# A two-layer trunk on one core: order of vector work at the start of each FFN, two sums of weights formed by an adding DMA, and one negative mean less per norm

## The chip, the cores and the metric

One core of a Trainium2 chip runs the whole program in one launch. The metric is the device time in microseconds (us). Three runs of the kernel before gave 2072.91, 2076.62 and 2079.84 us; the median is 2076.62.

## The reference, cut to what matters

Batch 1, 512 tokens, width 1024, float32, two layers. Each layer is a half-step SwiGLU FFN, a token mixer (layer 0: native sparse attention, NSA; layer 1: the gated linear recurrence HGRN2), and a second half-step FFN. A post-norm follows each of the six blocks:

```
for i in range(2):
    x = layer_norm(alpha*x + 0.5*swiglu(x, w_gate1, w_up1, w_down1))
    x = layer_norm(alpha*x + mixer_i(x))
    x = layer_norm(alpha*x + 0.5*swiglu(x, w_gate2, w_up2, w_down2))
swiglu(x, g, u, d) = (silu(x @ g) * (x @ u)) @ d        # 1024 -> 2816 -> 1024
```

## The kernel before, in words

Tokens lie in four chunks of 128 (c = 0 to 3); the model width in eight slices of 128 (k). Matmuls run in the fp32r format, and to keep float32 accuracy each operand is split into a high part (a rounded copy, made by ScalarE, line 123) and a low part (the difference, made by VectorE, line 124). A product of two split operands is three matmuls (`mm3`, lines 140 to 142). x stands transposed in SBUF as `xh` and `xl`.

The order of TensorE's instructions is the order of the code. The order on VectorE, ScalarE, GpSimd and in the DMA queues is made by a planner that lists the instructions by their place in the code and by when it thinks that they can start. The helper `after(ins)` tells the planner that what is traced inside it comes behind `ins` on the engine of each of `ins`.

**A norm** (`ln_tok`, lines 216 to 243) takes chunk c: two adds to x with bn_stats (lines 223, 224), bn_aggr (225), the negative mean `nm`, named lm, on GpSimd (227), 1/sqrt(var) by two GpSimd instructions (212, 213), and then the two half rows. The second half of chunks 0 to 2 goes through ScalarE (which takes `nm` as its bias) and GpSimd; everything else is two VectorE instructions per half (238, 239). In chunk 3 nothing reads `nm`. `finish` (245) runs the last matmuls of a block chunk by chunk with the norms behind them, and transposes chunks 0 and 1 for the next block meanwhile; chunks 2 and 3 stay in `pending` and are flushed by the next block.

**An FFN** (`ffn_body`, line 273) has 11 pairs of 128-column blocks of gate and up weights. Pair 0 is done plainly (`plain_pair`): first all products with tokens of chunks 0 and 1, in four parts, with the flush (transpose on TensorE, high part on ScalarE, low part on VectorE: `to_xt`) of chunk 2 ahead of the third part and of chunk 3 ahead of the fourth; then all products with chunks 2 and 3. Pairs 1 to 10 are done by `seven`: a Strassen-like scheme with 7 instead of 8 block products. It needs sums of blocks of x (`token_forms`, lines 189 to 200: four VectorE instructions of 128x512 for each of chunks 2 and 3, traced right behind the low part in `to_xt`, then split into t0, t1, t2) and sums of weight blocks. For pair g the gate and up weights come by four DMAs of 512 KB into two `fr` tiles (three buffers), called r0 and r1 here; a00, a10 are the column halves of r0 and a01, a11 those of r1. VectorE makes three sums into `raw` tiles (three buffers, shared with all weights that are loaded raw) and one in place, all at line 387:

```
s3 = a00 - a10;  s1 = a10 + a11;  s2 = a11 - s3 (into a10);  t = a01 - s2
w1 = parts(a00), w7 = parts(s3), w6 = parts(s2), w2 = parts(a01)
w5 = parts(s1),  w4 = parts(a11), w3 = parts(t)
```

`parts` is the split into high and low part. TensorE then takes products 1, 7, 6, 2, 5, 4, 3. Product 3 adds into bank e, which `c = e + p1` on VectorE (line 442) must have read first. The next pair's r1 needs an `fr` buffer of this pair; the last reader of both is the sum t. In the first FFN alone, pair 1's vector and scalar instructions already stand behind the flush of chunk 3.

Of the kernel before, what the change touches and what calls it, by code (L numbers as in the profile page):

```python
# [10 lines left out]
F32 = mybir.dt.float32  # L11
# [4 lines left out]
ALU = mybir.AluOpType  # L16

P = 128
# [3 lines left out]
NT = T // P  # L22
# [23 lines left out]

NSTD = 1

PLACE = 64

PSC = 4
# [10 lines left out]
class Trunk:  # L62
    def __init__(self, ctx, tc, a):
        self.tc, self.nc, self.a = tc, tc.nc, a
        nc = self.nc
        self.cst = ctx.enter_context(tc.tile_pool(name="cst", bufs=1))
        self.act = ctx.enter_context(tc.tile_pool(name="act", bufs=1))
        self.ident = self.cst.tile([P, P], F32, name="ident")
        make_identity(nc, self.ident)

        self.gap(self.cst, 128)
        self.mhalf = self.cst.tile([P, NT], F32, name="mhalf")
        nc.vector.memset(self.mhalf, -0.5)
        self.x = [self.act.tile([P, D], F32, name=f"x{c}") for c in range(NT)]

        self.raw = ctx.enter_context(tc.tile_pool(name="raw", bufs=3, reuse_waits="tile"))
        self.wr = ctx.enter_context(tc.tile_pool(name="wr", bufs=5, reuse_waits="tile"))
        self.xt = None
        self.pending = {}
        self.nxt, self.early, self.forms = None, [], None  # L80

    def gap(self, pool, n):
        pool.tile([P, n // 4], F32, name="gap")
# [93 lines left out]
    def to_xt(self, c):  # L177
        for h in range(2):
            p = self.psum().rearrange("p (k t) -> p k t", k=4)
            for j in range(4):  # L180
                k = 4 * h + j
                self.nc.tensor.transpose(p[:, j, :], self.x[c][:, k * P : (k + 1) * P], self.ident)
            s, t = slice(4 * h, 4 * h + 4), slice(c % 2 * P, c % 2 * P + P)
            ins = self.split(self.xh[:, c // 2, s, t], self.xl[:, c // 2, s, t], p)
            if self.forms is not None and c >= 2:
                self.token_forms(h, t, p)
        return ins

    def token_forms(self, h, t, p):
# [26 lines left out]
    def ln_tok(self, c, banks, gb, eps, out=None, scale=1.0):  # L216
        nc = self.nc
        x = self.x[c]
        st = self.small.tile([P, 2, 6], F32, name="st", tag="st")
        mv = self.small.tile([P, 2], F32, name="mv", tag="mv")  # L220
        for h in range(2):
            s = slice(512 * h, 512 * h + 512)
            nc.vector.scalar_tensor_tensor(x[:, s], x[:, s], float(scale), banks[h], op0=ALU.mult, op1=ALU.add)  # L223
            nc.vector.bn_stats(st[:, h, :], x[:, s])  # L224
        nc.vector.bn_aggr(mv, st.rearrange("p a b -> p (a b)"))
        nm = self.small.tile([P, 1], F32, name="lm", tag="lm")
        nc.gpsimd.tensor_scalar(nm, mv[:, 0:1], -1.0, None, op0=ALU.mult)
        r = self.rsqrt(mv[:, 1:2], 1, eps)
        for h in range(2):
            s = slice(512 * h, 512 * h + 512)  # L230

            if h == 1 and c < NT - 1:
                nc.scalar.activation(x[:, s], x[:, s], AF.Identity, bias=nm)
                nc.scalar.activation(x[:, s], x[:, s], AF.Copy, scale=r)
                nc.gpsimd.tensor_tensor(x[:, s], x[:, s], gb[0][:, s], op=ALU.mult)
                nc.gpsimd.tensor_tensor(x[:, s], x[:, s], gb[1][:, s], op=ALU.add)
            else:
                nc.vector.scalar_tensor_tensor(x[:, s], x[:, s], mv[:, 0:1], gb[0][:, s], op0=ALU.subtract, op1=ALU.mult)
                nc.vector.scalar_tensor_tensor(x[:, s], x[:, s], r, gb[1][:, s], op0=ALU.mult, op1=ALU.add)
            if out is not None:  # L240
                nc.sync.dma_start(out[0, c * P : (c + 1) * P, s], x[:, s])
        if out is None:
            self.pending[c] = partial(self.to_xt, c)
# [29 lines left out]
    def ffn_body(self, pool, wg, wu, wd, gb_idx, out):  # L273
        nc = self.nc
        self.gap(pool, 128)
        h = pool.tile([P, 12, T], F32, name="h")

        self.wx = pool, 2
        w3 = [w.rearrange("(k p) f -> p k f", p=P) for w in (wg, wu)]
        LASTU = 4  # L280
        with ExitStack() as es:
            mid = es.enter_context(self.tc.tile_pool(name="mid", bufs=1, reuse_waits="tile"))
            self.gap(mid, 192)
            tf = [[mid.tile([P, 4, 256], F32R, name=f"t{n}{x}") for x in "hl"] for n in range(3)]

            hq = h.rearrange("p j t -> p (j t)")
            xb = hq[:, 2048:4096].rearrange("p (a k t) -> p a k t", a=2, k=4)
            f1, f2 = (hq[:, 1024 * n : 1024 * n + 1024].rearrange("p (k t) -> p k t", k=4) for n in (4, 5))
            for half, (f0, nf) in enumerate(((0, 12), (12, 10))):
                for pr in range(nf // 2):  # L290
                    g = f0 // 2 + pr
                    if g < NSTD:
                        if g == 0:
                            for k in range(2):
                                ks = slice(4 * k, 4 * k + 4)
                                nc.vector.tensor_tensor(xb[:, k], self.xh[:, 0, ks].bitcast(F32), self.xl[:, 0, ks].bitcast(F32), op=ALU.add)
                            self.forms = xb, f1, f2
                        self.plain_pair(mid, w3, g, h[:, 2 * pr : 2 * pr + 2, :])
                        if g == 0:
                            self.forms = None  # L300
                            for (hi, lo), src in zip(tf, (f1, f2, xb[:, 0])):
                                self.split(hi, lo, src)
                        if g == NSTD - 1:
                            self.split(self.xh[:, 1, 0:4], self.xl[:, 1, 0:4], xb[:, 1])
                    else:

                        with self.after(self.flushed if g == NSTD and gb_idx == (0, 0) else ()):
                            self.seven(mid, tf, w3, g, h[:, 2 * pr : 2 * pr + 2, :], 1 if g < NSTD + 2 else 2 if half == 1 and pr == 0 else 0)
                if half == 0:
                    banks = self.down(wd, h, f0, nf, nf, None)  # L310
                    for c in range(NT):
                        for x in range(2):
                            s = slice(512 * x, 512 * x + 512)
                            nc.vector.scalar_tensor_tensor(self.x[c][:, s], self.x[c][:, s], 2.0 * ALPHA, banks[c][x], op0=ALU.mult, op1=ALU.add)
        with ExitStack() as es:
            wl = es.enter_context(self.tc.tile_pool(name="wl", bufs=4, reuse_waits="tile"))
            gb = self.ln_params(*gb_idx, [wl.tile([P, D], F32, name=n, bufs=1) for n in ("lng", "lnb")])
            banks, last = self.down(wd, h, f0, nf, nf - LASTU, wl)
            self.finish(last, banks, gb, 4.0 * LN_EPS, out)
# [49 lines left out]
    def seven(self, pool, tf, w3, g, h, wide):  # L369
# [3 lines left out]
        nc = self.nc  # L373
# [3 lines left out]
        for kk in range(2):  # L377
            t = pool.tile([P, 2, 4, 256], F32, name="fr", tag="fr", bufs=3)
# [3 lines left out]
        a00, a10, a01, a11 = r[0][..., :P], r[0][..., P:], r[1][..., :P], r[1][..., P:]  # L382

        def form(x, y, op, out=None):
            if out is None:
                out = self.raw.tile([P, 2, 4, P], F32, name="raw", tag="raw")
            tt(out, x, y, op=op)  # L387
            return out
# [8 lines left out]

        w = {1: parts(a00)}
        s3 = form(a00, a10, ALU.subtract)
        s1 = form(a10, a11, ALU.add)  # L400
        s2 = form(a11, s3, ALU.subtract, a10)
        w[7] = parts(s3)
        w[6] = parts(s2)
# [16 lines left out]
        c = pool.tile([P, 2, 2, 256], F32, name="c")  # L420
# [841 lines left out]
def body(ctx, tc, a, out):  # L1262
# [14 lines left out]

    for r, t.nxt, t.place in zip(run, first[1:] + [None], (PLACE, 0, 0, PLACE, 0, 0)):
        r()
# [25 lines left out]
```

## Time and profile before

| what | us |
|---|---|
| runs, median of 3 (lowest, highest) | 2076.62 (2072.91, 2079.84) |
| the profiled execution, its own time | 2074.36 |
| its span from first to last instruction | 2072.6 |

The profiled execution lies 2.26 us under the median of the runs. In the span TensorE is shown busy for 99%, at full clock (mean granted 0.999). The four FFNs start at about 9, 703, 1046 and 1730 us.

How to read it: times in rows are us from the span's start. In a timeline a row is start, duration, engine, line, operation, out<-in, shapes, count, and in brackets the idle time before it with what ended it. Merged rows (x2) carry the start of the first. VectorE instructions overlap by some 0.08 us, so back-to-back ones start 0.60 us (128x512) or 1.14 us (128x1024) apart while the row says 0.68 or 1.22.

### The profile page before, as it was taken

Reading aid. Unit: us, or ns where it says so; the run is one execution under the profiler, and the core shown is the slowest. Engines: PE = TensorE matmul, PEld = TensorE weight load, DVE = VectorE, ACT = ScalarE, POOL = GpSimd, SP = SyncE. Lnnn points to the kernel's source line nnn. Section 1 sums busy time; section 2 is a strip of 40 time slices with the busy share of each in tenths; the row PEclk is TensorE's granted clock in tenths of the full one; section 3 lists DMA queues with packets and bytes.
Section 4 is the critical chain, followed back from the end, with each engine's and each line's share of the span. In section 5 each row is a group of like instructions: output and inputs, shape, how many; then the busy total and the mean of one; then the engine's idle time right before and its main releaser. Section 6 shows DMA issues by size and latency. Waiting matters only on the chain.

```text
span 2072.6 us, 34647 instructions
## 1 busy us (share of the span) xinstructions
PE 2045.6 (99%) x14329; PEld 1879.6 (91%) x14329; DVE 1402.1 (68%) x2108; ACT 988.2 (48%) x1594; POOL 197.1 (10%) x313
## 2 busy tenths in 40 slices
PE   9999999999999999999999999999999999999998
PEld 9998998889999899899899989988888989998996
DVE  8846865367776796486598468654647859855864
ACT  5543552355665355255345435524736735542551
POOL 0000002001112200000110000030421212000002
PEclk9999999999999999999999999999999999999999
DMA  5341342341101145133234413523230022442331
GB/s 183 123 149 56 103 144 74 89 111 34 40 32 52 62 123 163 41 103 106 97 102 131 145 51 102 163 63 96 88 119 31 2 72 76 130 162 61 103 123 41
DMA packets 138762, 194.00 MB, mean 94 GB/s; under 512 B 8571, under 2 KB 117435, under 8 KB 138604
## 3 DMA queue, kind: packets, MB, share of 16 engines
q1 hardware_dynamic: 138604, 191.79, 29.8%
q8 instruction: 112, 1.84, 0.4%
q14 instruction: 46, 0.38, 0.1%
HBM read 189.58 MB, written 2.19 MB: 93 GB/s over the span
## 4 chain that ended last, share of the span: by engine, by line
PE 84%; DVE 9%; ACT 3%; POOL 2%; issue 1%; DMA 1%; SPq 0%; POOLq 0%; DVEq 0%; ACTq 0%
PE ps L140 23%; PE ps L142 23%; PE ps L141 23%; PE po L851 3%; PE ps L835 2%; DVE wlo L124 1%; PE ps L1187 1%; PE ps L356 1%; DVE raw L387 1%; DMA fr<-in_ffn_w_up_dram 1%; DVE st L224 1%; PE sc L803 1%; PE sc L802 1%; DVE x L223 1%; PE ps L574 1%
## 5 line engine op out<-in xcount | busy, mean ns | idle before, releaser
L124 DVE TENSOR_TENSOR wlo<-raw,whi 128x1024 fp32r<-128x1024 f32 (+1 forms) x253 | 311.2, 1234 | 259.7 <-ACT whi L123 259.2
L123 ACT ACTIVATE whi<-raw 128x1024 fp32r<-128x1024 f32 (+1 forms) x253 | 265.9, 1056 | 335.7 <-PE ps L142 157.0
L141 PE MATMUL ps<-xl,whi 128*128 128x256 f32 (+1 forms) x992 | 293.6, 296 | 2.7 <-DVE xl L124 2.7
L140 PE MATMUL ps<-xh,whi 128*128 128x256 f32 (+1 forms) x992 | 294.5, 297 | 1.1 <-ACT xh L123 0.5
L142 PE MATMUL ps<-xh,wlo 128*128 128x256 f32 (+1 forms) x992 | 293.2, 296 | 0.0
L142 PE MATMUL ps<-whi,xlo 128*128 128x512 f32 x704 | 274.5, 390 | 1.5 <-DVE xlo L124 1.5
L140 PE MATMUL ps<-whi,xhi 128*128 128x512 f32 x704 | 274.5, 390 | 0.0
L141 PE MATMUL ps<-wlo,xhi 128*128 128x512 f32 x704 | 274.0, 389 | 0.0
L141 PEld LDWEIGHTS ps<-xl,whi 128*128 128x128 f32 x992 | 186.8, 188 | 9.9 <-DVE xl L124 3.5
L140 PEld LDWEIGHTS ps<-xh,whi 128*128 128x128 f32 x992 | 186.6, 188 | 8.7 <-ACT xh L123 1.0
L142 PEld LDWEIGHTS ps<-xh,wlo 128*128 128x128 f32 x992 | 186.3, 188 | 6.4
L123 ACT ACTIVATE whi<-fr 128x1024 fp32r<-128x1024 f32 x120 | 126.7, 1061 | 129.7 <-PE ps L141 80.4
L140 PE MATMUL ps<-xh,xhi 128*128 128x256 f32 x640 | 177.8, 278 | 3.1 <-DVE c L442 3.1
L124 DVE TENSOR_TENSOR wlo<-fr,whi 128x1024 fp32r<-128x1024 f32 x120 | 146.1, 1219 | 46.7 <-ACT whi L123 46.7
L141 PE MATMUL ps<-xl,xhi 128*128 128x256 f32 x640 | 177.5, 277 | 0.0
L142 PE MATMUL ps<-xh,xlo 128*128 128x256 f32 x640 | 177.4, 277 | 0.0
L387 DVE TENSOR_TENSOR raw<-fr 128x1024 f32<-128x1024 f32 x120 | 145.8, 1219 | 21.7 <-DMA fr<-in_ffn_w_up_dram 20.3
L142 PEld LDWEIGHTS ps<-whi,xlo 128*128 128x128 f32 x704 | 132.2, 188 | 30.6 <-DVE xlo L124 3.2
L141 PEld LDWEIGHTS ps<-wlo,xhi 128*128 128x128 f32 x704 | 132.2, 188 | 27.0
L140 PEld LDWEIGHTS ps<-whi,xhi 128*128 128x128 f32 x704 | 132.2, 188 | 26.8
L124 DVE TENSOR_TENSOR xlo<-h,xhi 128x1024 fp32r<-128x1024 f32 x44 | 53.9, 1226 | 112.8 <-ACT xhi L123 112.8
L140 PEld LDWEIGHTS ps<-xh,xhi 128*128 128x128 f32 x640 | 120.4, 188 | 3.7 <-DVE c L442 3.7
(270 smaller groups left out, 4865.5 us busy)
## 6 DMA issues: line engine op xcount, KB each, us to landing
raw<-in_ffn_w_down_dram SPq DMA_DIRECT2D x88, 512.0 KB, 3.5
fr<-in_ffn_w_gate_dram SPq DMA_DIRECT2D x80, 512.0 KB, 4.0
fr<-in_ffn_w_up_dram SPq DMA_DIRECT2D x80, 512.0 KB, 5.1
raw<-in_hgrn_w_in_dram SPq DMA_DIRECT2D x32, 512.0 KB, 4.1
raw<-in_nsa_w_in_dram SPq DMA_DIRECT2D x18, 512.0 KB, 4.0
raw<-in_ffn_w_gate_dram SPq DMA_DIRECT2D x8, 512.0 KB, 5.3
raw<-in_ffn_w_up_dram SPq DMA_DIRECT2D x8, 512.0 KB, 4.7
raw<-in_nsa_w_out_dram SPq DMA_DIRECT2D x8, 512.0 KB, 3.5
```

The costliest lines, as they stand in the source:

```text
L123: a = self.nc.scalar.activation(hi, src, AF.Copy)
L124: b = self.nc.vector.tensor_tensor(lo, src, hi.bitcast(F32), op=ALU.subtract)
L140: mm(out, l[0], r[0], start=start, stop=False)
L141: mm(out, l[0], r[1], start=False, stop=False)
L142: mm(out, l[1], r[0], start=False, stop=stop)
L223: nc.vector.scalar_tensor_tensor(x[:, s], x[:, s], float(scale), banks[h], op0=ALU.mult, op1=ALU.add)
L224: nc.vector.bn_stats(st[:, h, :], x[:, s])
L356: nc.tensor.matmul(out, l, xx, start=k == low == 0 and xx is x[0], stop=k == 7 and low == 1)
L387: tt(out, x, y, op=op)
L574: nc.tensor.matmul(ph, w1[:, j, :], self.ap(z[:, 0:1], 2 * j, [[16, 129]]), start=j == 0, stop=j == 15)
L835: nc.tensor.transpose(p[:, j * P : j * P + P], pf[:, (b0 + j) * P : (b0 + j + 1) * P], self.ident)
L851: nc.tensor.matmul(po[:, ii, t, :], pt[:, t * (i + 1) + j, :], v[j][:, t, g, :], start=j == 0, stop=j == i)
```

## The change

Four edits. (1) In an FFN's pair 0 the sums of `token_forms` are collected in `late` and traced behind the low part of chunk 3's second half, on VectorE. (2) Pair 1's vector and scalar instructions stand behind the flush of chunk 3 in all four FFNs, not only in the first. (3) In pairs 1 and 2 of the FFNs other than the first, s1 is not made by VectorE: its `raw` tile is loaded by two SP DMAs (a10 of gate and of up, rows of 128 columns, 256 KB each) and two DMAs issued by GpSimd that add a11 (256 KB each). (4) `nm` is not made for chunk 3.

```diff
+ACCUM = 1, 2
...
-        self.nxt, self.early, self.forms = None, [], None
+        self.nxt, self.early, self.forms, self.late = None, [], None, []
...
             if self.forms is not None and c >= 2:
-                self.token_forms(h, t, p)
+
+                self.late.append(partial(self.token_forms, h, t, p))
+        if c == NT - 1 and self.late:
+            with self.after(ins):
+                for f in self.late:
+                    f()
+            self.late = []
         return ins
...
         nc.vector.bn_aggr(mv, st.rearrange("p a b -> p (a b)"))
-        nm = self.small.tile([P, 1], F32, name="lm", tag="lm")
-        nc.gpsimd.tensor_scalar(nm, mv[:, 0:1], -1.0, None, op0=ALU.mult)
+        if c < NT - 1:
+            nm = self.small.tile([P, 1], F32, name="lm", tag="lm")
+            nc.gpsimd.tensor_scalar(nm, mv[:, 0:1], -1.0, None, op0=ALU.mult)
...
         self.gap(pool, 128)
+        self.accum = ACCUM if gb_idx != (0, 0) else ()
...
-                        with self.after(self.flushed if g == NSTD and gb_idx == (0, 0) else ()):
+                        with self.after(self.flushed if g == NSTD else ()):
...
         s3 = form(a00, a10, ALU.subtract)
-        s1 = form(a10, a11, ALU.add)
+        if g in self.accum:
+
+            s1 = self.raw.tile([P, 2, 4, P], F32, name="raw", tag="raw")
+            fs = slice(2 * g * P + P, 2 * g * P + 2 * P)
+            for m, src in enumerate(w3):
+                nc.sync.dma_start(s1[:, m], src[:, 0:4, fs])
+                nc.gpsimd.dma_start(s1[:, m], src[:, 4:8, fs], accum_op=ALU.add)
+        else:
+            s1 = form(a10, a11, ALU.add)
         s2 = form(a11, s3, ALU.subtract, a10)
```

## Rows read from the trace of the kernel before

**Rows 1.** The page's first part: busy time, share of the span and instructions of TensorE, its weight loads, VectorE, ScalarE and GpSimd.

```profile
PE 2045.6 (99%) x14329; PEld 1879.6 (91%) x14329; DVE 1402.1 (68%) x2108; ACT 988.2 (48%) x1594; POOL 197.1 (10%) x313
```

**Rows 2.** TensorE's waits over the whole span, the largest entry: line, what it waited for, us in total, times, longest.

```profile
PE ps L140 <- DVE c L442: 3.1, 3, 1.3
```

**Rows 3.** TensorE's timeline, the six matmuls at the FFN starts with over 0.5 us idle ahead of them.

```profile
51.55 0.39 PE L140 MATMUL ps<-xh,xhi 128*128 128x256 f32 x1 [1.34 <-DVE c L442]
...
717.78 0.39 PE L141 MATMUL ps<-xl,whi 128*128 128x256 f32 x1 [1.34 <-DVE xl L124]
...
729.65 0.73 PE L431 MATMUL ps<-xh,whi 128*128 128x512 f32 x2 [0.83 <-ACT xh L123]
...
747.52 0.39 PE L140 MATMUL ps<-xh,xhi 128*128 128x256 f32 x1 [0.81 <-DVE c L442]
...
1738.93 0.38 PE L141 MATMUL ps<-xl,whi 128*128 128x256 f32 x1 [0.66 <-DVE xl L124]
...
1767.81 0.39 PE L140 MATMUL ps<-xh,xhi 128*128 128x256 f32 x1 [0.94 <-DVE c L442]
```

**Rows 4.** Busy time of the engines in one stretch, the third FFN's start: stretch, length, busy us (instructions) of TensorE, its weight loads, VectorE, ScalarE and GpSimd, granted clock, DMA share, GB/s.

```profile
1046.00:1087.00 41.00, 40.99 (x352) 40.86 (x353) 39.20 (x46) 20.50 (x26) 2.00 (x3) 1.00 0.41 129
```

**Rows 5.** Timelines of VectorE (DVE) and ScalarE (ACT) at the second FFN's start: the low part of pair 1's w1; chunk 2's first low part; the high parts of chunk 3; chunk 3's first low part; pair 1's t; pair 2's s1 and s2; and c.

```profile
711.17 1.22 DVE L124 TENSOR_TENSOR wlo<-fr,whi 128x1024 fp32r<-128x1024 f32 x1
712.31 0.68 DVE L124 TENSOR_TENSOR xl<-ps,xh 128x512 fp32r<-128x512 f32 x1
...
713.19 1.09 ACT L123 ACTIVATE xh<-ps 128x512 fp32r<-128x512 f32 x2 [0.54 <-PE ps L182]
...
717.04 0.68 DVE L124 TENSOR_TENSOR xl<-ps,xh 128x512 fp32r<-128x512 f32 x1
...
734.35 1.22 DVE L387 TENSOR_TENSOR raw<-fr 128x1024 f32<-128x1024 f32 x1
...
741.78 1.23 DVE L387 TENSOR_TENSOR raw<-fr 128x1024 f32<-128x1024 f32 x1 [1.53 <-DMA fr<-in_ffn_w_up_dram]
743.04 1.23 DVE L387 TENSOR_TENSOR fr<-fr,raw 128x1024 f32<-128x1024 f32 x1
...
746.79 0.68 DVE L442 TENSOR_TENSOR c<-ps,p 128x512 f32<-128x512 f32 x1
```

**Rows 6.** The same two timelines at the first FFN's start: chunk 2's first low part; chunk 3's high parts; pair 1's t; pair 2's s1; c.

```profile
16.36 0.68 DVE L124 TENSOR_TENSOR xl<-ps,xh 128x512 fp32r<-128x512 f32 x1
...
18.65 1.09 ACT L123 ACTIVATE xh<-ps 128x512 fp32r<-128x512 f32 x2 [2.52 <-PE ps L182]
...
39.64 1.22 DVE L387 TENSOR_TENSOR raw<-fr 128x1024 f32<-128x1024 f32 x1
...
48.21 1.23 DVE L387 TENSOR_TENSOR raw<-fr 128x1024 f32<-128x1024 f32 x1 [2.73 <-DMA fr<-in_ffn_w_up_dram]
...
50.82 0.68 DVE L442 TENSOR_TENSOR c<-ps,p 128x512 f32<-128x512 f32 x1
```

**Rows 7.** The same two timelines at the starts of the third and the fourth FFN: chunk 2's first low part, chunk 3's high parts, pair 1's t, pair 2's s1, and c, for each.

```profile
1052.48 0.68 DVE L124 TENSOR_TENSOR xl<-ps,xh 128x512 fp32r<-128x512 f32 x1
...
1054.92 1.09 ACT L123 ACTIVATE xh<-ps 128x512 fp32r<-128x512 f32 x2 [2.52 <-PE ps L182]
...
1075.84 1.22 DVE L387 TENSOR_TENSOR raw<-fr 128x1024 f32<-128x1024 f32 x1
...
1082.65 1.23 DVE L387 TENSOR_TENSOR raw<-fr 128x1024 f32<-128x1024 f32 x1 [0.97 <-DMA fr<-in_ffn_w_up_dram]
...
1085.26 0.68 DVE L442 TENSOR_TENSOR c<-ps,p 128x512 f32<-128x512 f32 x1
...
1733.46 0.68 DVE L124 TENSOR_TENSOR xl<-ps,xh 128x512 fp32r<-128x512 f32 x1
...
1735.02 1.09 ACT L123 ACTIVATE xh<-ps 128x512 fp32r<-128x512 f32 x2 [1.57 <-PE ps L182]
...
1756.64 1.22 DVE L387 TENSOR_TENSOR raw<-fr 128x1024 f32<-128x1024 f32 x1
...
1764.46 1.23 DVE L387 TENSOR_TENSOR raw<-fr 128x1024 f32<-128x1024 f32 x1 [1.98 <-DMA fr<-in_ffn_w_up_dram]
...
1767.07 0.68 DVE L442 TENSOR_TENSOR c<-ps,p 128x512 f32<-128x512 f32 x1
```

**Rows 8.** Timelines of GpSimd (POOL) and VectorE at the end of the program, the last norm's chunk 3, with the same GpSimd add of chunk 2 as the first row.

```profile
2061.24 0.21 POOL L212 TENSOR_SCALAR ry<-mv 128x1 f32<-128x1 f32 x1
...
2065.93 0.78 POOL L227 TENSOR_SCALAR lm<-mv 128x1 f32<-128x1 f32 x1 [0.36 <-DVE mv L225]
2066.68 0.69 POOL L212 TENSOR_SCALAR ry<-mv 128x1 f32<-128x1 f32 x1
2067.45 0.57 POOL L213 TENSOR_TENSOR ry<-ry,mhalf 128x1 f32<-128x1 f32 x1
...
2068.05 1.41 DVE L239 SCALAR_TENSOR_TENSOR x<-x,ry,lnb 128x512 f32<-128x512 f32 x2 [0.76 <-POOL ry L213]
```

**Rows 9.** The raw tiles: an issue of a raw load for HGRN in the view of that tile (line, queue, operation, count, durations, first and last start), the time from issue to landing over all raw loads, and GpSimd's idle time ahead of the norm that comes before the second FFN.

```profile
L994 SPq DMA_DIRECT2D raw<-in_hgrn_lb_dram x1: 344/344/344, 1344.1 to 1344.1; - x1
...
DMA to landing us min/median/max: 2.1/3.7/8.4
...
686.61 0.79 POOL L227 TENSOR_SCALAR lm<-mv 128x1 f32<-128x1 f32 x1 [25.67 <-DVE mv L225]
```

## The prediction

> **What bounds the kernel now.** I read the page's first part, then TensorE's waits, then its timeline at the FFN starts. TensorE is busy for 2045.6 [rows 1] of the span's 2072.6 us, so only its idle time can be won. Its largest wait is for c (line 442) [rows 2]. At the four FFN starts (A, B, C, D from here on, at about 9, 703, 1046 and 1730 us) six matmuls have over 0.5 us idle ahead of them [rows 3]: 1.34 in A; 1.34 (chunk 3's low part), 0.83 (the high part of the sum x4) and 0.81 (c) in B; 0.66 (low part) and 0.94 (c) in D. That is 5.92 us. C has none: 40.99 of 41.00 us are busy [rows 4]. So all that the change can win at FFN starts is 5.92 us, 0.29% of the time.
>
> The timelines of VectorE and ScalarE show what makes them. VectorE works without a break from chunk 2's low part until pair 2's s1, which waits 0.97 to 2.73 us for a DMA [rows 5 to 7]. That DMA brings pair 2's r1, which waits for the buffers that pair 1's sum t releases; c stands behind s1 and s2 of pair 2. The chain is: VectorE's burst, t, DMA, s1, s2, c, product 3. A wait of TensorE ahead of this chain costs nothing in the end if c is late anyway. This is where the change is to be weighed.
>
> **The change part by part.** Steps of VectorE, start to start: 1.14 us for 128x1024 (711.17 to 712.31, where the row says 1.22: 0.08 of overlap), so 0.60 for a 128x512 of 0.68 [rows 5].
>
> *Low parts first, sums late.* The low parts of chunk 3 can only follow its high parts, and these follow transposes whose place on TensorE does not move. In B the high parts start at 713.19, the first is done half of 1.09 later at 713.74, so chunk 3's two low parts end at 713.74 + 1.20 = 714.94. TensorE's wait for them until 717.78 [rows 3] ends. But the sums of chunk 2, which filled VectorE before, must now stand behind 714.94 too, as must pair 1's weight work, so VectorE has a hole. What t then does, for each start [rows 5 to 7]:
> - A: before, from the low part at 16.36 to t's end 39.64 + 1.14 = 40.78 are 24.42 us. Without the four low parts (2.40) 22.02 remain, now from 18.65 + 0.55 + 1.20 = 20.40: t ends at 42.42, 1.64 later. Nothing in A gives this back: no adding DMA there, and no nm ahead of it.
> - B: from pair 1's w1 low part at 711.17, which stood ahead, to 735.49 are 24.32, less 2.40, less s1 (1.14): 20.78 from 714.94, t ends at 735.72, 0.23 later.
> - C: 1052.48 to 1076.98 are 24.50, less 2.40 and 1.14: 20.96 from 1054.92 + 1.75 = 1056.67, t ends at 1077.63, 0.65 later.
> - D: 1733.46 to 1757.78 are 24.32, less 3.54: 20.78 from 1736.77, t ends at 1757.55, 0.23 earlier.
> Pair 2's r1 lands later or earlier by as much. The transposed banks are held longer by the sums, until 4.80 us behind the low parts; the next taker of banks is pair 1, some 11 us behind, so that costs nothing.
>
> *Sums by adding DMAs.* Each takes one 128x1024 off VectorE. Pair 1's is counted above. Pair 2's stands directly in the chain: s2 need not wait for it. So c in B comes at 746.79 + 0.23 - 1.26 = 745.76 (s1 to s2 took 1.26 [rows 5]), 1.03 earlier; in C at 1085.26 + 0.65 - 1.14 = 1084.77, still no wait; in D at 1767.07 - 0.23 - 1.14 = 1765.70, 1.37 earlier. In A c is 1.64 later. On the queues: 12 more DMAs on SP at some 0.34 us of issue [rows 9] and 12 on GpSimd. No row has a DMA issued by GpSimd or an adding one. Bounds for one: the raw loads land in 2.1 to 8.4 us, median 3.7 [rows 9]; an add reads and writes, so I take twice the median, 7.4, behind its load's 3.7. That is 11.1 us per tile, at nothing if it is covered. The cover: raw loads are not bound to their place in the code, since HGRN's load at line 994 goes out at 1344.1, while the FFN ahead of HGRN still runs [rows 9]. With raw buffers free early I expect both sums of a start to be loaded before the norm, where GpSimd idles 25.67 us [rows 9]. Without that cover see the third rival.
>
> A DMA from GpSimd has a rule against it here. VectorE is busy 39.20 of 41.00 us at a start [rows 4]. The Trainium skill, "SBUF — State Buffer", section "SBUF: two separate sides", says that the descriptors of such a DMA are written by GpSimd, which is locked out while VectorE runs an operation that takes both ports. By the rule a transfer issued inside the burst would stall, giving the third rival's time; issued ahead of it, the forecast's. No run so far shows which.
>
> *Weights behind the flush.* In B, C, D it only moves VectorE and ScalarE work, counted above. ScalarE's high parts have idle time around them (0.54 to 2.52 us ahead of chunk 3's alone [rows 5 to 7]).
>
> *No nm.* At FFN starts nothing: the hole waits for chunk 3's high parts anyway. At the end it lies on the path. The add after nm took 0.69 us beside VectorE's two-input instruction against 0.21 behind one [rows 8]; GpSimd seems held until VectorE's instruction is over. If that holds, the power ends at best 0.57 behind the last such instruction, which ended 0.76 ahead of 2068.05, at 2067.29: 2067.86, and 0.17 is won. If not, all 0.76 of VectorE's wait. I take 0.40.
>
> **The sum.** A +1.64, B -1.03, C 0, D -1.37, end -0.40: -1.16, say -1.2. On the profiled execution's 2074.36 that is 2073.2; on the median of the runs, which is 2.26 above, 2075.4. Bounds: A from -1.34 (c placed ahead of the late sums) to +1.64; B from -2.98 to 0; D from -1.60 to 0; end -0.76 to -0.17. The parts' ends are not reached together; with some 2 us of scatter of a median the case's own range is 2072 to 2078.
>
> **The rivals.** About 0.3% (6.2 us) is what a measurement of this kernel can tell from no change.
> 1. *All waits go* (chance 0.17). The planner orders VectorE; if it puts c ahead of pair 2's late sums, c waits for no DMA and TensorE meets none of the six waits: -5.92 and -0.76 at the end, -6.7, 2069.9. For it: low parts are in time by over 2 us in B and nothing else binds. Against: before, it chose s2 first in every start.
> 2. *The planner puts c further back* (0.13, the slower side). In A, C and D c starts 2.61 behind pair 2's s1, in B 5.01 [rows 5 to 7]: there two more operations stand ahead of c. If the shifted work makes the planner choose B's order everywhere, c is 2.40 later in A, C and D: A +4.04; C 1084.77 + 2.40 = 1087.17 against the 1085.26 that just sufficed, +1.9; D +1.03; B -1.03; end -0.40. That is +5.5, 2082.1. It decides where c stands two places behind the first that it could take.
> 3. *The adding DMAs come late* (0.07). If they stand ahead of chunk 3's power on GpSimd's queue, or starve in VectorE's burst, VectorE, in order, stops at w5 or TensorE at the transposes; I price one median load, 3.7, per start: three times 3.7, less 1.2: +9.9, 2086.5. Against it: the idle GpSimd and the early raw loads.
> The forecast's case has 0.63.
>
> **How the numbers follow.** Faster by over 6.2 us: half of rival 1 and a little scatter, 0.11. Slower by over 6.2 us: rival 3 and a third of rival 2, 0.11. The rest, 0.78, is within. Range: from the first rival's time to just under the second's, 2069.8 to 2081.5, which leaves out rival 3 and parts of the others, under 0.2.
>
> **What would show it.** In the profile after: chunk 3's low parts in B end near 715 with a hole of VectorE ahead of them; TensorE's waits for low parts at 717.78 and 1738.93 are gone; t in A ends near 42.4 and TensorE's wait for c there grows from 1.34 to about 3; the waits for c in B and D move rather than vanish; GpSimd's DMAs stand ahead of the norms; the last power ends 0.2 to 0.7 earlier. Wrong would be: a wait for s1's tile anywhere, c placed elsewhere, or a wait in C.

## The result and the profile after

The changed kernel took 2088.84 us (median of 5 runs, 2084.42 to 2092.65) against 2076.62: a ratio of 1.0065, 95% interval 1.0049 to 1.0080. It is slower, by 12 us in the medians, where no change was forecast (2075.4, range 2069.8 to 2081.5). Its profiled execution took 2084.42 us, with a span of 2082.6: 10.0 us longer than that of before.

TensorE's waits first. Columns: what waited and what it waited for, us in total, times, longest.

```profile
PE ps L142 <- ACT ps L451: 9.5, 4, 4.5
...
PE ps L142 <- DVE c L460: 1.1, 1, 1.1
...
PE ps L143 <- DVE xl L126: 0.7, 2, 0.3
```

The waits for c are down from 3.1 us in three places [rows 2] to one of 1.1, and no low part of x is waited for at an FFN start any more (the two waits in the last row lie elsewhere). A new wait is larger than all that: for line 451, ScalarE's copy of bank a into bank b behind product 1. TensorE's timeline shows where: at product 6 of pair 2 in B (4.50 us of idle time), C (2.73) and D (2.13).

```profile
758.25 0.58 PE L142 MATMUL ps<-t1h,whi 128*128 128x256 f32 x1 [4.50 <-ACT ps L451]
...
1101.53 0.39 PE L142 MATMUL ps<-t1h,whi 128*128 128x256 f32 x1 [2.73 <-ACT ps L451]
...
1785.60 0.58 PE L142 MATMUL ps<-t1h,whi 128*128 128x256 f32 x1 [2.13 <-ACT ps L451]
```

Why the copy is late stands on ScalarE's timeline in B.

```profile
742.16 2.01 ACT L125 ACTIVATE whi<-fr 128x1024 fp32r<-128x1024 f32 x2 [2.58 <-DVE fr L397]
753.03 1.06 ACT L125 ACTIVATE whi<-raw 128x1024 fp32r<-128x1024 f32 x1 [8.85 <-DMA raw<-in_ffn_w_up_dram]
753.99 1.04 ACT L125 ACTIVATE xhi<-fr 128x1024 fp32r<-128x1024 f32 x1
...
757.61 0.58 ACT L451 ACTIVATE ps<-ps 128x512 f32<-128x512 f32 x1
```

ScalarE stands for 8.85 us at the high part of w5, whose source is pair 2's s1, the tile that two transfers now make. It runs in order: the high part of w4, c's silu, three more instructions and the copy come behind. The DMA issues tell when the tile was made. SP's queue first (L390 is the load of `fr` tiles, L415 that of a10 into s1's tile), then GpSimd (L416 adds a11):

```profile
735.37 0.37 SPq L390 DMA_DIRECT2D fr<-in_ffn_w_gate_dram  x1
735.78 0.51 SPq L390 DMA_DIRECT2D fr<-in_ffn_w_up_dram  x1
736.45 0.39 SPq L415 DMA_DIRECT2D raw<-in_ffn_w_gate_dram  x1
736.88 0.51 SPq L415 DMA_DIRECT2D raw<-in_ffn_w_up_dram  x1
```

```profile
742.98 1.28 POOL L416 DMA_DIRECT2D raw<-in_ffn_w_gate_dram  x1 [25.18 <-DMA raw<-in_ffn_w_gate_dram]
743.73 1.83 POOL L416 DMA_DIRECT2D raw<-in_ffn_w_up_dram  x1
```

r1 (735.37) goes out when the sum t of pair 1, ended at 735.31, has freed its buffer. s1's loads stand behind it on SP's queue and behind its 1 MB on the transfer engines; the adding transfers wait for the loads until 742.98. The DMA view of 743 to 753.1 us (queue: packets, MB, share of the 16 engines; issues: KB, us to landing) gives the last leg: 4.7 and 9.2 us.

```profile
q1 hardware_dynamic: 1661, 1.64, 54.4%
q0 software_dynamic: 1056, 0.52, 42.0%
...
raw<-in_ffn_w_gate_dram POOLq DMA_DIRECT2D x1, 256.0 KB, 4.7
raw<-in_ffn_w_up_dram POOLq DMA_DIRECT2D x1, 256.0 KB, 9.2
```

743.73 + 9.2 is 752.9, and 753.03 is when ScalarE goes on. From the first issue at 736.45 the tile took 16.5 us. GpSimd's 0.52 MB took 42.0% of the engines' time, SP's 1.64 MB (the end of pair 3's r0 and then its r1, which interleave with it; pair 2's r1 had landed by 740.90) 54.4%. The Trainium skill, "DMA: Bandwidth & Descriptors", section "Issuing engines are not separate DMA queues", says that transfers started by different engines run on the same 16 DMA engines and interleave; this trace agrees.

One more loss follows from the idle time. Columns of the stretches: length, busy us (instructions) of TensorE, weight loads, VectorE, ScalarE and GpSimd, granted clock, DMA share, GB/s.

```profile
753.40:758.20 4.80, 0.34 (x3) 0.14 (x2) 3.84 (x5) 4.79 (x7) 0.00 (x0) 0.99 0.00 1
758.20:761.60 3.40, 3.35 (x16) 3.35 (x17) 3.40 (x4) 1.47 (x2) 0.00 (x0) 0.51 0.85 253
761.60:765.00 3.40, 3.40 (x33) 3.40 (x32) 3.40 (x4) 1.53 (x3) 0.00 (x0) 1.00 0.17 55
```

Behind the idle 4.5 us the granted clock is at half (1.2 of 2.4 GHz) for 3.4 us, and TensorE does 16 matmuls where the next 3.4 us hold 33. C and D have the same behind their waits; the kernel before had none at an FFN start. Less some waiting for c that it hides, a stretch costs at most 17 times 0.11 us, 1.9 us. In the other four runs the mean granted clock was 0.993 to 0.995 against 0.997 in the profiled one, and 0.998 or so for the kernel before. That means more time at half clock, which fits a median 4.4 us above the profiled execution. Where it lay is not shown: the profiles of some kernels below have such stretches outside of the FFN starts too (6.83 us at 652.7 in the one with the filled waits).

### The profile page after: what moved, and what is told of

Same layout as the page of the kernel before. It is cut to its first block, busy times and chain, and to the rows that moved or that the text cites. A ratio compares the mean times of both kernels' runs of the same rounds, so it can differ in the third digit from the quotient of the medians.

```text
span 2082.6 us, 34706 instructions
## 1 busy us (share of the span) xinstructions
PE 2049.0 (98%) x14329; PEld 1882.6 (90%) x14329; DVE 1398.2 (67%) x2102; ACT 987.2 (47%) x1594; POOL 212.0 (10%) x319
## 3 DMA queue, kind: packets, MB, share of 16 engines
q0 software_dynamic: 6336, 3.15, 1.2%
## 4 chain that ended last, share of the span: by engine, by line
PE 84%; DVE 7%; ACT 3%; DMA 3%; issue 1%; POOL 1%; SPq 0%; POOLq 0%; DVEq 0%; ACTq 0%
PE ps L142 23%; PE ps L144 23%; PE ps L143 23%; PE po L869 3%; PE ps L366 2%; PE ps L853 2%; PE ps L1205 1%; DVE wlo L126 1%; DMA raw<-in_ffn_w_up_dram 1%; DMA fr<-in_ffn_w_up_dram 1%; PE sc L821 1%; PE sc L820 1%; PE ps L184 1%; PE ps L592 1%; DVE raw L397 1%
## 5 line engine op out<-in xcount | busy, mean ns | idle before, releaser
L397 DVE TENSOR_TENSOR raw<-fr 128x1024 f32<-128x1024 f32 x114 | 138.3, 1222 | 21.9 <-DMA fr<-in_ffn_w_up_dram 20.5
```

## The experiments

My theory, once the result was read: pair 2's sum lands late, because its transfers stand behind r1 and the adding ones are slow; ScalarE's queue carries the delay to TensorE; the half clock comes from the idle time. The main rival: the new order itself (low parts first, sums and weights behind the flush) is late for its consumers. All ratios are against the kernel before, run beside each kernel on the same chip. Times of different kernels that are set side by side below are from the span's start; B starts at 702.63 in the changed kernel, at 702.25 with plain copies and at 706.03 with the early sums.

**The adding transfers alone**, on the kernel before:

```diff
+ACCUM = 1, 2
...
-        s1 = form(a10, a11, ALU.add)
+        if g in self.accum:
+            ...   # the two SP loads and two adding transfers of the change
+        else:
+            s1 = form(a10, a11, ALU.add)
```

> The kernel before with the adding transfers of pairs 1 and 2 and nothing else of the change. Late-transfer theory: the loss comes with it in full: pair 2's s1 lands 15 to 17 us behind the start of its pair's r1 transfer whatever the order of the sums, TensorE idles 2 to 5 us in three starts with a stretch at half clock behind each; 0.4 to 0.9% slower than before, 2084 to 2095. Rival, loss from the new order or from both together: within 0.2% of before.

Measured 2089.26 us, ratio 1.0072 (1.0059 to 1.0084): the whole loss without the rest of the change. TensorE's largest wait is again for the copy, which is line 444 here:

```profile
PE ps L142 <- ACT ps L444: 10.5, 3, 5.0
```

**No adding transfer, the rest kept:**

```diff
-ACCUM = 1, 2
+ACCUM = ()
```

> The changed kernel with VectorE making s1 in every pair again: no adding transfer, the order of the sums, of the weight work and the missing negative mean kept. Late-transfer theory: all that the change loses comes from pair 2's s1, which lands behind ScalarE's need of it; without it the waits for the copy of line 451 (10.2 us with the one of 0.46) and the three stretches at half clock (1.7 us each) go, and the 0.6 us that the first FFN's start gained and 0.3 us at the end stay: 0.1 to 0.3% faster than before, 2071 to 2075. Rival, the new order itself loses (sums and weight work behind the flush are late for products 7 and 6): still slower than before by 0.2% or more, above 2081, with waits of TensorE for ScalarE or VectorE at the second to fourth FFN start.

2077.57 us, ratio 1.0016 (1.0004 to 1.0027). Both theories missed: the 10 us are gone, but no gain is left. The profile says what eats it: in B, C and D TensorE waits for weight low parts in pair 1 (0.5 to 0.7 us each), and for c in pairs 2 and 3 (4.4 us in six places, A's included).

```profile
PE ps L142 <- DVE c L460: 4.4, 6, 1.0
```

With s1 back on VectorE, the new order makes it late for its consumers: in this much the rival holds.

**Adding transfers in pair 1 alone:**

```diff
-ACCUM = 1, 2
+ACCUM = (1,)
```

> The changed kernel with the adding transfers in pair 1 alone. Late-transfer theory: pair 1's tile was in time (its high part at 728.87 waited for no DMA that TensorE felt), so no wait for the copy of line 451 and no stretch at half clock before the end: within 1.5 us of the kernel without adding transfers, 2070 to 2075, and VectorE's t of pair 1 about 1.1 us earlier than there. Rival, any adding transfer costs (it holds SP's queue and shares the transfer engines with r1 of pair 2): s2 of pair 2 waits longer for its DMA than 0.6 us, c is late, and the time lies 3 us or more above the kernel without.

2075.82 us, ratio 1.0007 (0.9999 to 1.0016). No wait for the copy, no wait for c of over 0.25 us in B, C and D, no half clock at an FFN start. Pair 1's transfer is harmless and takes waits away; pair 2's makes the loss. But TensorE's gaps in B, C and D (those of over 0.25 us, from matmul to matmul and beyond the usual spacing) fell from 5.8 us in the kernel before to 1.9, and the median did not follow. That is taken up below.

**Is it the addition, or the place in the chain?** The adding transfers as plain copies, so that this kernel leaves the addition out of s1:

```diff
-                nc.gpsimd.dma_start(s1[:, m], src[:, 4:8, fs], accum_op=ALU.add)
+                nc.gpsimd.dma_start(s1[:, m], src[:, 4:8, fs])
```

> The changed kernel with GpSimd's transfers as plain copies: the addition in s1 is left out, so the tile holds a11 alone; issue, queue, bytes and waits are kept. If the addition makes the transfer slow: the 512 KB of a pair take some 3.0 us as the plain rows of SP's queue did (739.65 to 742.69) in place of 4.2 to 7.5, pair 2's high part of w5 starts 1.5 to 4 us earlier and the waits for the copy of line 451 shrink to under half, 4 to 8 us faster than the changed kernel. If instead the place in the chain does it (issued behind SP's load, which stands behind r1; 2.0 to 2.3 us from issue to the first packet; shared engines): the tile lands within 1 us of where it did, and the time is that of the changed kernel within 2 us.

2077.39 us, ratio 1.0006 (0.9993 to 1.0019): some 12 us faster than the changed kernel by the ratios, more than expected. GpSimd issues at the same time as before, but the transfers of pair 2 in B land in 4.2 and 4.3 us instead of 4.7 and 9.2, and the high part of w5 starts at 747.67 instead of 753.03. GpSimd's rows, ScalarE's row and the two rows of the DMA view of 735 to 755 us:

```profile
742.51 0.75 POOL L416 DMA_DIRECT2D raw<-in_ffn_w_gate_dram  x1 [26.22 <-DMA raw<-in_ffn_w_gate_dram]
743.25 0.75 POOL L416 DMA_DIRECT2D raw<-in_ffn_w_up_dram  x1
```

```profile
747.67 1.06 ACT L125 ACTIVATE whi<-raw 128x1024 fp32r<-128x1024 f32 x1 [3.86 <-DMA raw<-in_ffn_w_up_dram]
```

```profile
raw<-in_ffn_w_gate_dram POOLq DMA_DIRECT2D x1, 256.0 KB, 4.2
raw<-in_ffn_w_up_dram POOLq DMA_DIRECT2D x1, 256.0 KB, 4.3
```

The page's third part, GpSimd's queue over the whole span (packets, MB, share of 16 engines), of the changed kernel and then of this one:

```profile
q0 software_dynamic: 6336, 3.15, 1.2%
```

```profile
q0 software_dynamic: 960, 3.15, 0.5%
```

The same bytes go in 6336 small packets at over twice the engines' time. So the loss needs the addition's price. It also needs the place of the transfers, as the next kernel shows; to take away either is enough.

**The place in the chain.** s1's four transfers are written ahead of r1's:

```diff
         for kk in range(2):
+            if kk == 1 and g in self.accum:
+                s1 = self.raw.tile([P, 2, 4, P], F32, name="raw", tag="raw")
+                ...   # the two SP loads and two adding transfers, as in the change
             t = pool.tile([P, 2, 4, 256], F32, name="fr", tag="fr", bufs=3)
```

> The changed kernel with s1's four transfers written ahead of r1's in each of the two pairs, so that on SP's queue pair 2's loads no longer stand behind r1's, which wait for the sum t at 735.3. They then wait only for their buffer, free when pair 1's w5 is split (about 731). Queue theory: issue near 731 instead of 736.5, landed and added by about 742 to 745 instead of 752.5, before ScalarE comes to w5; waits for the copy of line 451 and half-clock stretches gone; within 2 us of the kernel with adding transfers in pair 1 alone (2075.8). Rival, the addition competes with r1 for the transfer engines, r1 lands 2 to 3 us later, and s2, t and c of pair 2 with it: c is waited for 1 to 3 us per start, 2079 to 2084.

2072.53 us, ratio 0.9987 (0.9977 to 0.9998), a little under the expected 2073.8 to 2077.8: the queue theory holds. The adding transfers are as slow to issue as before; those of pair 2 in B land in 5.7 and 6.3 us. SP's rows of B (L392 is s1's load, here of pair 1 and then of pair 2; L396 that of `fr`) and GpSimd's:

```profile
680.37 0.37 SPq L392 DMA_DIRECT2D raw<-in_ffn_w_gate_dram  x1
...
731.32 0.37 SPq L392 DMA_DIRECT2D raw<-in_ffn_w_gate_dram  x1
...
738.77 0.37 SPq L396 DMA_DIRECT2D fr<-in_ffn_w_gate_dram  x1
```

```profile
684.19 1.49 POOL L393 DMA_DIRECT2D raw<-in_ffn_w_gate_dram  x1 [22.62 <-issue]
...
735.01 1.36 POOL L393 DMA_DIRECT2D raw<-in_ffn_w_gate_dram  x1 [25.06 <-DMA raw<-in_ffn_w_gate_dram]
```

Pair 1's sum is now made ahead of the norm. Pair 2's loads go out at 731.32 instead of 736.45 (25.3 us behind B's start instead of 33.8). They do not go earlier, because they wait for a raw buffer, which VectorE's reading of another raw tile frees at 731.29. ScalarE does not wait for them: w5's high part stands right behind the one before. The rival is there in small: c is waited for 2.0 us in all, 0.8 at most.

```profile
749.01 1.05 ACT L125 ACTIVATE whi<-raw 128x1024 fp32r<-128x1024 f32 x1
```

```profile
PE ps L142 <- DVE c L459: 2.0, 4, 0.8
```

**The clock.** The waits are filled with dummy matmuls:

```diff
         product(7, d, True)
+        for _ in range(self.fill if g == 2 else 0):    # 21, 13, 10 in B, C, D
+            nc.tensor.matmul(e, w[1][0][:, 0, 0, :], self.xr(0)[0], start=True, stop=True, skip_group_check=True)
         product(6, b, False)
```

> The changed kernel with 21, 13 and 10 dummy matmuls (128x512, 0.21 us each at full clock) ahead of pair 2's product 6 in the second, third and fourth FFN: they fill the waits of 4.78, 3.01 and 2.40 us with work that is overwritten. If the stretches at half clock come from TensorE's idle time, they go, and with them 3 times 1.7 us, while the copy of line 451 ends where it did: 5 us (0.25%) faster than the changed kernel in the profiled execution, and more in the median, whose granted clocks were lower. If the half clock has another cause (the transfers, the time since the start), the stretches stay and the time is that of the changed kernel or up to 1 us longer. If the half clock explains nothing of the loss, no difference over 1 us.

2086.01 us, ratio 1.0055 (1.0041 to 1.0069). The first half of the theory holds, the gain does not come: the granted clock stays full behind all three fills, yet the time can't be told from the changed kernel's 1.0065.

```profile
759.00:762.50 3.50, 3.50 (x30) 3.36 (x29) 3.47 (x4) 1.19 (x2) 0.00 (x0) 1.00 0.94 294
1104.00:1108.00 4.00, 4.00 (x32) 3.77 (x31) 3.97 (x6) 2.40 (x3) 0.00 (x0) 1.00 0.65 204
1787.00:1791.00 4.00, 4.00 (x31) 3.79 (x30) 4.00 (x5) 2.61 (x4) 0.00 (x0) 1.00 0.53 154
```

One reason is a fault of the experiment: the fill was sized by the old waits, but here the planner moved the copy ahead of one high part. In B the dummies ran from 754.66 for 5.06 us while the copy (now line 452) ended at 757.67, so the fill itself was 2.05 us too long; in C it was 1.41 and in D 0.72 us too long. What the half clock costs in a run is therefore bounded by its rows (at most 1.9 us a stretch), not measured.

**What is left of the change: three starts, two starts, and once more.** Pair 1's transfer alone, with the first FFN as before:

```diff
+ACCUM = (1,)
+STARTS = ((0, 2), (1, 0), (1, 2))
...
+        self.defer = gb_idx in STARTS
+        self.accum = ACCUM if self.defer else ()
...
-                self.late.append(partial(self.token_forms, h, t, p))
+                if self.defer:
+                    self.late.append(partial(self.token_forms, h, t, p))
+                else:
+                    self.token_forms(h, t, p)
...
```

> Adding transfers in pair 1 alone, the new order in the second to fourth FFN alone, no negative mean in chunk 3; the first FFN as before. Counting TensorE's idle time over 0.25 us in the starts: 1.99 us in A as before, 0.64 in each of the others instead of 3.47, 0 and 2.31: 3.9 us less, and 0.3 at the end: 4 us (0.2%) faster than before, if idle time is all that counts. Spacing theory: in one start the matmuls follow each other in 0.113 or 0.118 us, chosen anew at a gap and kept to the next, worth up to 3.8 us a start whatever the kernel; then the runs scatter as those of before and the median lies 0 to 4 us under it, but the profile, less its slow spacing, lies 4 us under that of before, less its own. If the new order keeps the slow spacing more often (both of the starts without a later gap had it), no gain or a loss up to 2 us, and C and D have it again.

2069.30 us, ratio 0.9973 (0.9960 to 0.9987). With `STARTS = ((0, 2), (1, 2))`:

> As the kernel with three starts, but the third FFN is as before too: new order and pair 1's adding transfer in the second and fourth FFN alone. Idle time: 0.64 less per gained start in C, so 4.9 us in all under before if idle time is all that counts; 0.6 us under the kernel with three starts. If the new order itself keeps the slow spacing, this kernel gains on the other by up to 2 us.

2073.32 us, ratio 0.9996 (0.9985 to 1.0006): 4 us above the kernel with three starts, where 0.6 to 2 us under it was expected, though it has the least idle time of all. And the kernel with three starts unchanged, in a later measurement on another chip:

> The kernel with three starts once more, word for word, for its ratio and for a second look at the spacing of its matmuls. If the gain is real and the rest chance: between 0.2% and 0.4% faster than before, and the spacing of the second to fourth start (fast, part slow, slow in the first look) falls out otherwise. If the spacing is fixed by the order of instructions: the same three again.

2075.24 us, ratio 1.0019 (1.0008 to 1.0029). The expectation of a real gain falls: the same instructions gave 0.9973 and 1.0019, and the two intervals do not meet. Whether that comes from the chip or from one measurement to the next is not shown. Two stretches of the first measurement's profile, then of the second's, in which TensorE never stops and the granted clock is full:

```profile
90.00:120.00 30.00, 30.00 (x267) 30.00 (x266) 20.89 (x22) 16.58 (x22) 0.00 (x0) 1.00 0.57 174
1785.00:1840.00 55.00, 55.00 (x469) 55.00 (x468) 38.80 (x41) 29.31 (x40) 0.00 (x0) 1.00 0.50 158
```

```profile
90.00:120.00 30.00, 30.00 (x257) 30.00 (x257) 20.38 (x22) 15.54 (x21) 0.00 (x0) 1.00 0.52 159
1785.00:1840.00 55.00, 55.00 (x487) 54.99 (x486) 40.54 (x43) 30.57 (x42) 0.00 (x0) 1.00 0.54 164
```

267 matmuls in 30 us or 257, 487 in 55 us or 469 (those that reach into a stretch count too): the matmuls of `seven` follow each other in 0.1134 or in 0.1178 us, and which of them changes from execution to execution. In the profiles a spacing mostly lasts from one gap of TensorE to the next, at most 840 matmuls, 3.7 us a start. The table sets it apart for all profiles (those of the last two rows are told of below). "Starts" is the sum over A to D of the time from pair 0's first matmul to the first of the down projection; "slow" is what matmuls in the longer spacing took beyond 0.1133 us each.

| kernel | starts | slow | starts less slow | ratio of runs |
|---|---|---|---|---|
| before | 495.8 | 7.9 | 487.9 | 1 |
| after | 504.9 | 5.3 | 499.5 | 1.0065 |
| adding alone | 509.8 | 5.4 | 504.4 | 1.0072 |
| wait filled | 507.4 | 9.1 | 498.3 | 1.0055 |
| no adding | 499.2 | 6.9 | 492.3 | 1.0016 |
| pair 1 alone | 495.4 | 10.8 | 484.5 | 1.0007 |
| plain second | 491.9 | 1.6 | 490.3 | 1.0006 |
| early sum | 489.3 | 3.3 | 486.0 | 0.9987 |
| three starts | 491.3 | 7.5 | 483.8 | 0.9973 |
| the same again | 494.9 | 11.9 | 483.0 | 1.0019 |
| two starts | 496.5 | 15.9 | 480.6 | 0.9996 |
| short ones | 490.3 | 8.2 | 482.1 | 0.9984 |
| both early, three starts | 491.2 | 2.9 | 488.3 | 0.9999 |

Without the slow part the two profiles of the same kernel agree within 1 us. The five profiles with next to no waits in B, C and D (pair 1 alone, three starts twice, two starts, short ones) lose 7.5 to 15.9 us to the spacing, the eight others 1.6 to 9.1. In three of the five the starts are within 1 us of the kernel before: what the waits gave back went there. In the other two they are 4.5 and 5.5 us shorter. That fits a spacing which lasts until the next gap. Why it should be so is only argued: in the fast spacing TensorE would come earlier to product 3 and so have a gap there. A does not show that. It has the same instructions in the kernels before, with three starts, two starts and short ones, and in all their profiles the matmuls of pair 1 run in the longer spacing (from 34 to 50 us). Where a wait for c of 0.9 to 1.3 us follows at about 51, the next matmuls run in the shorter one, to 64 at least; where no wait follows (two starts, short ones), the longer one stays to the end, 4.0 and 4.1 us of loss. In these five profiles, then, the slow spacing ended at a gap, and the gap did not come from a fast one.

**Can the spacing be changed?** Two short matmuls ahead of pair 1's product 1, on the kernel with three starts:

```diff
+        for n in range(2 if g == NSTD and self.defer else 0):
+            nc.tensor.matmul(a[:, :P], w[1][0][:, 0, 0, :], self.xc(0, 0)[0], start=True, stop=True, skip_group_check=True)
         product(1, a, True)
```

> The kernel with three starts and two further matmuls of 128 columns ahead of pair 1's product 1 in each of them (overwritten; some 0.2 us a start). Chance theory: the spacing is chosen at the gap ahead of pair 1, and nothing behind it changes that; slow in about half of the starts, 0 to 1 us slower than the kernel with three starts. Rival: short matmuls let the weight loads get ahead, as behind the transposes of the flush, after which every start so far ran fast; then fast in all three, and 2 to 5 us faster than the kernel with three starts.

2068.66 us, ratio 0.9984 (0.9975 to 0.9993). Inconclusive: its profile has C fast throughout, B slow in the last 525 matmuls and D slow in the first 168, which is neither all fast nor clearly chance. Beside the kernel with three starts, measured on the same chip at the same time (2075.24), it is 6.6 us faster, more than the rival's 2 to 5; beside that kernel's first ratio, 0.9973, it is slower. A ratio of one measurement this near 1 settles nothing.

**Both transfers early, three starts:** the two edits above together.

> Both adding transfers, written ahead of r1, new order in the second to fourth FFN alone, the first as before. Queue theory: as the kernel with the early sums in four starts (0.9987 of before), less 0 to 1 us for the first start, 2070 to 2073; no wait for the copy of line 451 and no stretch at half clock behind one. Against the kernel with three starts and pair 1's transfer alone: pair 2's transfer gains VectorE 1.1 us that nothing waits for, while it delays r1 of pair 2 by 2 to 3 us (issued at 738.8 in place of 735.4 in the second FFN), so c is waited for 0.5 to 1 us a start: 1 to 3 us slower than that kernel.

2070.85 us, ratio 0.9999 (0.9991 to 1.0007), within the expected 2070 to 2073. No wait for the copy; c is waited for in pair 2 with gaps of up to 2.3 us from matmul to matmul, more than expected. Against the kernel with three starts the expectation missed: 4.4 us faster on the same chip, not 1 to 3 slower; its profile lost 2.9 us to the slow spacing, that one's 11.9. No version here, then, is shown to beat the kernel before by more than one measurement differs from another. The loss is another matter: the three kernels with both adding transfers behind r1 have 1.0055 to 1.0072, the eight other kernels 0.9973 to 1.0019.

## Why the prediction was wrong, step by step

**The step that failed is the cover of the adding transfers**: "With raw buffers free early I expect both sums of a start to be loaded before the norm". Pair 2's loads went out at 736.45, behind r1, which waits for the sum t. The wait for s1's tile, which I had named as a sign of being wrong, is the 8.85 us of ScalarE in B. I took one early load of another block (HGRN's, [rows 9]) as a rule. Writing the transfers ahead of r1 brought for pair 1 what I had expected, loads at 680.37 ahead of the norm, and took the loss away. For pair 2 the expectation could not come true even so: no raw buffer was free for it before 731.29. Pair 1's transfers were not ahead of the norm either in the changed kernel; GpSimd issued them in VectorE's burst:

```profile
714.99 1.49 POOL L416 DMA_DIRECT2D raw<-in_ffn_w_gate_dram  x1 [8.43 <-DMA raw<-in_ffn_w_gate_dram]
```

They were in time by the slack of their consumer: they had landed by 721.8, and the high part of pair 1's w5 starts at 728.87.

**The size failed too.** I bounded a tile by 11.1 us (3.7 and twice that); it took 16.5 in B. The loads took 6.5 of them, behind r1, and the adding transfers up to 9.2 where I had 7.4 as the upper end; copies without the addition took 4.3. Where less ran beside them, the adding ones kept my bound: 4.8 and 5.8 us in pair 1 of B, with SP's queue at 18.1% of the engines' time from 712 to 722.

**The consumer was followed on one engine alone.** "s2 need not wait for it" is right: s2 started at 740.90, before the adding transfers were issued. But w5's high part stands on ScalarE, and behind it the next copy on which TensorE's product 6 hangs. The third rival had the late transfer, with VectorE stopping at w5 and 3.7 us a start; its 2086.5 is the nearest of my times to 2088.84. Without the slow spacing the starts cost +3.3, +5.8 and +2.0 us in B, C and D. Its chance of 0.07 was too low: a cover that rests on one row of another block is no ground for so little.

**Not in the prediction at all**: the half clock behind the waits of 2.13 to 4.50 us.

**The rule on GpSimd's descriptors.** No run shows a stall. The adding transfers issued at 714.99 and 716.03, with VectorE busy all the time, took 1.49 and 1.78 us to issue and landed in 4.8 and 5.8 us; those issued at 684.19 and 685.23, ahead of the norm, in the kernel with the early sums took 1.49 and 1.78 and landed in 4.8 and 5.9. Plain ones at 742.51 and 743.25 took 0.75 us to issue and landed in 4.2 and 4.3. I had stretched the rule: the Trainium skill, "SBUF — State Buffer", section "SBUF: two separate sides", speaks of a VectorE operation in a mode that takes both ports. VectorE's rows in the burst are two-input TENSOR_TENSOR instructions, and nothing here shows them in such a mode, so no run here tries the rule itself.

**The steps of VectorE** were right in three starts of four. Rows of B:

```profile
713.26 1.29 DVE L126 TENSOR_TENSOR xl<-ps,xh 128x512 fp32r<-128x512 f32 x2 [1.65 <-ACT xh L125]
...
734.09 1.22 DVE L397 TENSOR_TENSOR raw<-fr 128x1024 f32<-128x1024 f32 x1
...
740.90 1.23 DVE L397 TENSOR_TENSOR fr<-fr,raw 128x1024 f32<-128x1024 f32 x1 [0.64 <-DMA fr<-in_ffn_w_up_dram]
742.16 1.23 DVE L397 TENSOR_TENSOR raw<-fr 128x1024 f32<-128x1024 f32 x1
743.31 0.68 DVE L460 TENSOR_TENSOR c<-ps,p 128x512 f32<-128x512 f32 x1
```

B starts 0.56 earlier than before, so 714.94 for the end of the low parts becomes 714.38, and they end at 713.26 + 1.20 = 714.46, with the hole ahead. t, forecast to end at 735.72 - 0.56 = 735.16, ends at 734.09 + 1.14 = 735.23. In C and D, shifted by their starts (3.60 and 8.06), t was due at 1081.23 and 1765.61 and ended at 1081.12 and 1765.69. The low-part waits are gone.

c in D was due at 1765.70 + 8.06 = 1773.76 and started at 1773.73, in part by luck: t stood between s2 and c, which I had not counted, and r1 landed some 1 us earlier than forecast. In C it came 0.8 later than due, with t between s2 and c, and in B 1.9 earlier, with t alone between them. TensorE waits for c in none of the three.

**A was wrong.** t was due at 42.42 + 0.75 = 43.17, since A starts 0.75 later, and ended at 38.76 + 1.14 = 39.90:

```profile
20.21 1.29 DVE L126 TENSOR_TENSOR xl<-ps,xh 128x512 fp32r<-128x512 f32 x2 [2.32 <-ACT xh L125]
...
38.76 1.22 DVE L397 TENSOR_TENSOR raw<-fr 128x1024 f32<-128x1024 f32 x1
39.90 2.36 DVE L126 TENSOR_TENSOR wlo<-fr,whi 128x1024 fp32r<-128x1024 f32 x2
42.17 1.22 DVE L126 TENSOR_TENSOR wlo<-raw,whi 128x1024 fp32r<-128x1024 f32 x1
```

The planner put three weight low parts, which stood ahead of t (36.23 to 39.64 in the trace of before), behind it. The wait for c of 1.34 us went and came back as 1.1 in pair 3, with 0.4 for one of those weight parts: without the slow spacing A costs +0.6 us, where I had +1.64.

**The end** gave 0.31 us of the 0.40. VectorE's aggregate to its last instructions takes 2.11 us (2075.73 to 2077.84) instead of 2.42. GpSimd's add is still held, 0.78 us; the power takes longer, 0.92 against 0.57 [rows 8], and VectorE still waits 0.46.

```profile
2076.02 0.78 POOL L220 TENSOR_SCALAR ry<-mv 128x1 f32<-128x1 f32 x1 [0.36 <-DVE mv L233]
2076.89 0.92 POOL L221 TENSOR_TENSOR ry<-ry,mhalf 128x1 f32<-128x1 f32 x1
```

```profile
2077.84 1.42 DVE L248 SCALAR_TENSOR_TENSOR x<-x,ry,lnb 128x512 f32<-128x512 f32 x2 [0.46 <-POOL ry L221]
```

**The sum**, as the two profiles have it: A +0.6, B +3.3, C +5.8, D +2.0, end -0.3, slow spacing -2.6 by chance, and +1.2 that is left over and not traced: 10.0 us of span.

## What to carry to other kernels

When work moves from an engine to a transfer, write down for that transfer what stands ahead of it on its issuing queue and what that waits for, what it reads behind, and, for the instruction that takes its result, the whole rest of that engine's queue: here a wait that VectorE could afford reached TensorE through ScalarE. A cover by an idle engine counts only if the queue lets the transfer go out in that time and a buffer is free for it; here the place in the code and the number of raw buffers decided that. And when a gain of 0.2% is at stake, measure the same kernel twice first, on more than one chip, and compare the stretches of its profile rather than one median.

## What the runs showed of the hardware

- An adding transfer of 256 KB from GpSimd in rows of 512 bytes took 4.5 to 9.2 us in pair 2 of the changed kernel and 4.8 and 5.9 us ahead of the norm, a plain one 4.2 to 4.4 in pair 2; the adding ones' queue took 1.2% of the engines' time against 0.5% for the same bytes, and GpSimd 1.28 to 1.83 us to issue one against 0.75 in that place.
- Behind 2.13 to 4.50 us of idle time TensorE ran at the lower of its clocks for 3.4 us (changed kernel); with dummy matmuls in that time it did not.
- In uninterrupted stretches at full granted clock the same matmuls ran 0.1134 or 0.1178 us apart (267 or 257 in 30 us, in two profiles of one kernel). What chooses the spacing stays open.
